# Gate's v with tokens stationary: rounded products of 512 features for the prompt, float32 visits for the samples

## The chip, the cores and the metric

One core of one Trainium2 chip runs the whole kernel. The time is device microseconds (us) of one execution; the median of three runs counts. A profile is one execution of its own, with its own time.

## What is computed

One inference step of a decoder layer for 256 prompt tokens and 64 sample tokens (8 sequences of 8), in float32. The tokens lie side by side as 320 columns. What concerns us is the first projection and the gate's v:

```python
h = rms_norm(x, p["norm_mix_pre"])
proj = h @ p["w_in"]                      # 2048 -> 9248 columns
a_u, a_v, z, xbc, dt_raw = ...            # a_v: 2048 columns
v = layer_norm(jax.nn.gelu(a_v, approximate=False), ln_g, ln_b)
...
s = jnp.einsum("hts,bnshd->bnthd", w, vp) + b_s
return u * s, v[:, start:]
```

v is needed with a token in each partition and its 2048 features along the row: the layer norm runs over the features, and the gate's product sums over tokens. After the mixer come a projection back, a norm, and a convolved feed-forward layer (2048 to 2 x 5632 and back to 2048) with a last norm and residual.

## The kernel before, in words

**Products.** A float32 weight block (a "slab", `slab`, L109) is loaded on SyncE's queue, rounded to float32r by ScalarE (`whi`, L124), and what the rounding lost is taken by VectorE (`wlo`, L125). The tokens are split in the same way into `hT[0]` and `hT[1]`. A product is then three float32r products: whi x hi, whi x lo, wlo x hi (`accumulate`, L132, its matmuls at L136 to L138). The weight block of 128 features is stationary and the 320 tokens move, so a result has features in the partitions and tokens along the row. 16 row blocks of 128 inputs (kt, `KD` = 16) are summed in one PSUM bank. Two pools hold the eight banks: `mm` with four, `ms` (`misc`) with four. Rounded weights have three buffers each (`whi`, `wlo`), raw slabs three (`wraw`).

**The first visit.** At the start nothing is loaded yet, so the kernel begins with ten products of ones (L69) and goes through kt from 0 to 15 with six feature blocks of v at once (768 columns, L684 on): four banks of `mm` and two of `ms`. For each kt the tokens are split (`x_ready`, L614, on ScalarE and VectorE), for kt below 4 the slab comes in two halves of 384 columns, and in between run the squares of x (`x_squares`), the loads for dt and, at kt 15, the root of the mean square (`root`, L633: token sums on TensorE at L638 and L640, then eleven small steps on VectorE) and the products for dt (`dt_products`, L492, at L497). The other ten feature blocks of v follow as three calls of `project` (L743 to L745).

**Turning v.** As features lie in the partitions, v has to be turned. `v_out` (L649) turns each finished bank in 32x32 blocks on VectorE (L653), and for each pair of blocks GpSimd's queue writes the turned rows to memory (L657). `v_in` (L663) is a side task: it loads the rows back by tokens on GpSimd's queue (L671), ScalarE applies the gelu with the token's root as its scale (L675) and writes `vt`, and VectorE gathers the statistics of the layer norm (L678). `layer_norm` (L747) waits until this task is done.

**Order.** The instructions of each engine stand in the order of the program except where a priority or `tc.issue_after` says otherwise; `tick` (L159) lets background tasks emit their next step between products, by counts of products made. `last_made` is the newest product on TensorE; with `issue_after(last_made[0])` an instruction stays behind it in its engine's order.

**The form that the change takes up.** In the down projection of the feed-forward layer the tokens are stationary already: `prompt_products` (L1509, matmul at L1513) has 128 tokens stationary and 512 rounded weight columns moving; `sample_products` (L1516, matmul at L1520) takes the 64 sample tokens unrounded, as true float32, against the raw weights, two products side by side in the two halves of the array's columns (`tile_position=(0, 64 * h)`). `samples()` calls it four times, with four products in each call.

**The end.** The last part of the down projection (`down_plain`, L1665) adds each finished bank to the sums (`joined`, L1671) on VectorE, takes squares on ScalarE, multiplies by the last norm's gain on GpSimd (`by_pool`, L1823) or VectorE (`by_gain`, L1815), and writes the result when a token's root is there. `last_sum` (L1833) is one more addition on VectorE; `one_block` (L1847) says which engine takes which gain. All of VectorE's steps there stand in the order of the code. Helpers record these steps at one line, L1806 for VectorE and L1810 for ScalarE.

Of the kernel before, what the change touches and what calls it, by code (L numbers as in the profile page):

```python
# [8 lines left out]
F32 = mybir.dt.float32  # L9
# [7 lines left out]
P = 128  # L17
NP = 256
# [15 lines left out]
def hybrid_step(  # L34
# [394 lines left out]
    with ExitStack() as mctx:  # L429
# [160 lines left out]
        with tc.tile_pool(name="gp", bufs=1) as gp:  # L590
# [23 lines left out]
            def x_ready(k0, nk):  # L614

                with tc.high_priority(offset=100000), tc.issue_after(rounded[0]) if rounded else nullcontext():
                    for kt in range(k0, k0 + nk):
                        x = xf[:, kt, :]
                        x_split.append(act.activation(hT[0][:, kt, :], x, AF.Copy, scale=pre[:, kt:kt + 1]).ins)
                        x_low.append(dve.scalar_tensor_tensor(out=hT[1][:, kt, :], in0=x, scalar=pre[:, kt:kt + 1],  # L620
                                                              in1=hT[0][:, kt, :].bitcast(F32), op0=ALU.mult, op1=ALU.subtract).ins)
# [25 lines left out]
            v_there = []  # L647

            def v_out(b, ps):  # L649

                t = turned[b // 2 % len(turned)]
                with first():
                    dve.transpose(out=t[:, :, b % 2], in_=ps[:, :NT].rearrange("p (s f) -> p s f", f=32))  # L653
                if b % 2:
                    for i in range(4):
                        rs = slice(32 * i, 32 * i + 32)
                        pool.dma_start(v_d[b // 2][:, 64 * i:64 * i + 64].rearrange("(s t) e -> t s e", t=32),  # L657
                                       t[rs].rearrange("p s j f -> p s (j f)"))
                    v_there.append(b // 2)

            bn = [gp.tile([P, 4, 6], F32, name=f"bn{c}") for c in range(3)]

            def v_in():  # L663

                for a in range(KD // 2):
                    while a not in v_there:
                        yield 24, 0
                    rows = []
                    for c, (o, n) in enumerate(TOK):
                        rows.append(tp.tile([P, NT], F32, tag="pv", name="v_rows", bufs=4)[:, :2 * P])  # L670
                        pool.dma_start(rows[c][:n], v_d[a][o:o + n])  # L671
                    yield 48, 0
                    with tc.issue_after(last_made[0]):
                        for c, (o, n) in enumerate(TOK):
                            func_ins.append(act.activation(vt[:n, c, 2 * P * a:2 * P * a + 2 * P].rearrange("p (j i f) -> p j i f", j=2, f=32),  # L675
                                                           rows[c][:n].rearrange("p (i j f) -> p j i f", j=2, f=32), AF.Gelu, scale=r[:n, c:c + 1]).ins)
                            if a % 2:
                                dve.bn_stats(bn[c][:n, a // 2, :], vt[:n, c, 256 * a - 256:256 * a + 256])  # L678
                    yield 0, 0
                with tc.issue_after(func_ins[-1]):  # L680
                    act.activation(held, ones[:, 0:1], AF.Silu)

            dt_loads = []
            ps = [mm.tile([P, 512], F32, tag="mm", name=f"ps_v{j}") for j in range(4)] + [misc(f"ps_v{j}") for j in (4, 5)]  # L684
            for kt in range(KD):
                x_ready(kt, 1)
                x = [h[:, kt, :] for h in hT]
                if kt < 4:
                    for g in range(2):
                        wb = slab(rows_of(w_in, kt, 1, V0 + 384 * g, 384), g, begins=kt + g == 0)  # L690
                        if kt == 0:
                            made_so_far[0] += 9
                            for i in (0, 2, 1):
                                for j in range(3):
                                    pe.matmul(ps[3 * g + j][:, :NT], wb(0, j)[i // 2], x[i % 2], start=i == 0, stop=False)
                        else:
                            for j in range(3):
                                accumulate(ps[3 * g + j][:, :NT], wb(0, j), *x, False, False)
                else:
                    wb = slab(rows_of(w_in, kt, 1, V0, 768))  # L700
                    for j in range(6):
                        accumulate(ps[j][:, :NT], wb(0, j), *x, False, kt == KD - 1)
                if 6 <= kt < 14:
                    with tc.issue_after(x_split[-1]):
                        x_squares(2 * (kt - 6))
                if kt in (8, 10):
                    dt_loads.append(dt_columns(kt // 10, gp))
                    next(dt_loads[-1])
                if kt in (12, 14):
                    with tc.issue_after(x_low[-1]):  # L710
                        next(dt_loads.pop(0), None)
                if kt == 15:
                    r = root()
                if kt == 15:
                    dt_products()
                if kt == 14:

                    with tc.issue_after(rounded[0]):
                        act.activation(held, ones[:, 0:1], AF.Gelu)
            turned = [gp.tile([P, 4, NT], F32, tag="vf", name="turned", bufs=2).rearrange("p j n -> p (j n)") for _ in range(2)]  # L720
            turned = [t[:, 2 * NT * h:2 * NT * h + 2 * NT].rearrange("p (s j f) -> p s j f", j=2, f=32) for t in turned for h in range(2)]
            for j in range(6):
                v_out(j, ps[j])
            for t, src in ((a_bc, ssm_a_log), (bias_bc, ssm_dt_bias)):

                pool.tensor_copy(t[:, 0:1], hT[0][:, 13, 0:1].bitcast(F32))
# [11 lines left out]
                next(tasks)  # L738
                yield 24, 0
            bg.append(with_r1())  # L740
            v_task = v_in()
            side.append(v_task)
            project(w_in, V0 + 768, lambda j, ps: v_out(6 + j, ps))  # L743
            project(w_in, V0 + 1280, lambda j, ps: v_out(10 + j, ps))
            project(w_in, V0 + 1792, lambda j, ps: v_out(14 + j, ps), width=256)  # L745

            def layer_norm():  # L747

                mv = gp.tile([P, 3, 2], F32, name="mv")
                pool.memset(mv, 1.0)  # L750
                while v_task in side:
                    yield 24, 0
# [558 lines left out]
    with tc.tile_pool(name="fp", bufs=1) as fp:  # L1311
# [353 lines left out]
        def down_plain(ck, parts, done, others):  # L1665
# [55 lines left out]
            for nb, i, w in sorted(later, key=lambda t: t[:2])[:-2]:  # L1721
                if i == 0:
                    ps = mm.tile([P, 512], F32, tag="mm", name=f"pd_{nb}_0")
                prompt_products(ps, x_of_tokens(0, i), w, i == 0, i == 1, True)
                if (nb, i) == (1, 1):
                    dve_add(f[0][1], ps)
                    samples_summed()
                    root(2, 0)
                    one_block(0, 1)
                    by_gain(2, 1)  # L1730
                    root(2, 1)
                    result(2, 0)
# [260 lines left out]
```

## Time and profile before

| | us |
|---|---|
| median of three runs | 1733.81 |
| lowest and highest | 1733.52, 1733.90 |
| the profiled execution | 1732.14 |
| its span in the trace | 1730.4 |
| busy: TensorE, VectorE, ScalarE, GpSimd | 1721.5, 1336.2, 878.6, 667.0 |

TensorE's granted clock was 0.999 over the span. How to read the lines that follow: a timeline row is start, duration, engine, line, operation, output and inputs with shapes; in brackets the idle time of the engine before it and what ended it. A row of the chain of waits is start, the time that it holds of the chain, and what. A row of the list of waits is who waited for whom, the total in us, how often, and the longest. Matmuls overlap in the pipeline, so the duration of one is longer than the distance to the next; distances of starts are the price. Rows of windows give, for each stretch, busy us (and instructions) of TensorE, its weight loads, VectorE, ScalarE and GpSimd, then the granted clock, the share of the DMA engines and GB/s.

### The profile page before, as it was taken

The numbers are of one execution on the slowest core, as the hardware profiler recorded it, in microseconds if no ns is written. First come the engines' busy times: TensorE is split into PE (matmuls) and PEld (weight loads), VectorE is DVE, ScalarE is ACT, GpSimd is POOL, SyncE is SP. The second block draws the span as 40 slices with busy tenths as digits, with TensorE's granted clock in tenths as the row PEclk, the third lists the DMA queues.
The fourth block names the chain that finished last, engine by engine and source line by source line (L and its number), as shares of the span: only waits on it lengthen the run. The fifth ranks groups of instructions, "written<-read, shape, count | busy, mean of one in ns | idle before, by whom it ended". The sixth has DMA issues, their size and how long they took to land.

```text
span 1730.4 us, 29959 instructions
## 1 busy us (share of the span) xinstructions
PE 1721.5 (99%) x11239; PEld 1608.1 (93%) x11239; DVE 1336.2 (77%) x2138; ACT 878.6 (51%) x1277; POOL 667.0 (39%) x1018
## 2 busy tenths in 40 slices
PE   9999999999999999999999999999999999999998
PEld 9999999999999999999998988989898989898985
DVE  7548864657869788788988878778787878697898
ACT  6344554333656565645655544444454544454554
POOL 2532230000414323112256546464545464555552
PEclk9999999999999999999999999999999999999999
DMA  8776655556676777665766454554545454545445
GB/s 263 219 236 189 186 173 152 156 161 186 204 227 198 227 218 218 203 208 165 224 190 216 122 177 136 170 153 155 165 143 161 138 170 135 174 134 172 135 152 156
DMA packets 216129, 310.07 MB, mean 179 GB/s; under 512 B 22064, under 2 KB 118960, under 8 KB 215792
## 3 DMA queue, kind: packets, MB, share of 16 engines
q1 hardware_dynamic: 198912, 280.02, 53.4%
q0 software_dynamic: 6144, 13.35, 2.7%
q10 hardware_dynamic: 10928, 14.79, 2.5%
q8 instruction: 88, 1.44, 0.3%
q14 instruction: 57, 0.47, 0.1%
HBM read 284.47 MB, written 22.32 MB: 177 GB/s over the span
## 4 chain that ended last, share of the span: by engine, by line
PE 98%; DVE 1%; DMA 0%; issue 0%; ACT 0%; DVEq 0%; SPq 0%; ACTq 0%
PE ps L136 21%; PE ps L138 20%; PE ps L137 20%; PE pm L1513 11%; PE pd L136 4%; PE pd L137 4%; PE pd L138 4%; PE pms L1520 4%; PE y_ps L1089 1%; PE ps_v L137 1%; PE ps_v L136 1%; PE ps_v L138 1%; PE yo_ps L1004 0%; PE up_ps L1021 0%; PE sg L811 0%; PE pd L1513 0%
## 5 line engine op out<-in xcount | busy, mean ns | idle before, releaser
L136 PE MATMUL ps<-h_hi,whi 128*128 128x320 f32 x2428 | 750.3, 309 | 0.0
L137 PE MATMUL ps<-h_lo,whi 128*128 128x320 f32 x2428 | 748.5, 308 | 0.0
L138 PE MATMUL ps<-h_hi,wlo 128*128 128x320 f32 x2428 | 748.3, 309 | 0.0
L125 DVE TENSOR_TENSOR wlo<-wraw,whi 128x1024 fp32r<-128x1024 f32 (+2 forms) x394 | 487.5, 1238 | 147.6 <-ACT whi L124 145.6
L124 ACT CAST whi<-wraw 128x1024 fp32r<-128x1024 f32 (+2 forms) x393 | 405.5, 1033 | 372.0 <-PE ps L137 143.8
L136 PEld LDWEIGHTS ps<-h_hi,whi 128*128 128x128 f32 x2428 | 455.6, 188 | 9.7 <-issue 1.3
L137 PEld LDWEIGHTS ps<-h_lo,whi 128*128 128x128 f32 x2428 | 455.9, 188 | 6.4
L138 PEld LDWEIGHTS ps<-h_hi,wlo 128*128 128x128 f32 x2428 | 455.5, 188 | 0.3
L136 PE MATMUL pd<-ohi,whi 128*128 128x320 f32 x448 | 138.7, 310 | 0.0
L138 PE MATMUL pd<-ohi,wlo 128*128 128x320 f32 x448 | 138.3, 309 | 0.0
L137 PE MATMUL pd<-olo,whi 128*128 128x320 f32 x448 | 138.3, 309 | 0.0
L1528 ACT CAST whi<-b 128x1024 fp32r<-128x1024 f32 x50 | 52.4, 1047 | 77.2 <-PE ps L137 56.6
L1376 POOL COPY ptf<-pad 128x2 f32<-128x2 f32 x88 | 41.8, 475 | 122.0 <-DVE pad L1358 120.3
L1529 DVE TENSOR_TENSOR wlo<-b,whi 128x1024 fp32r<-128x1024 f32 x50 | 65.2, 1303 | 29.6 <-ACT whi L1528 29.6
L136 PEld LDWEIGHTS pd<-ohi,whi 128*128 128x128 f32 x448 | 84.1, 188 | 0.6
L137 PEld LDWEIGHTS pd<-olo,whi 128*128 128x128 f32 x448 | 84.1, 188 | 0.3
L138 PEld LDWEIGHTS pd<-ohi,wlo 128*128 128x128 f32 x448 | 84.1, 188 | 0.0
L1551 POOL TENSOR_TENSOR one<-b,one 128x256 f32<-128x256 f32 x80 | 78.0, 1006 | 4.9 <-DVE wlo L1529 4.7
L249 DVE TENSOR_TENSOR acc_mix<-acc_mix,pd 128x320 f32<-128x320 f32 (+1 forms) x113 | 53.9, 480 | 28.2 <-PE pd L138 28.1
L1529 DVE TENSOR_TENSOR wlo<-one,whi 128x1024 fp32r<-128x1024 f32 x40 | 55.8, 1394 | 22.8 <-ACT whi L1528 22.7
L1520 PE MATMUL pms<-b,a_s 128*64 128x512 f32 x280 | 70.9, 596 | 0.0
L1528 ACT CAST whi<-one 128x1024 fp32r<-128x1024 f32 x40 | 41.8, 1045 | 57.0 <-PE ps L137 54.1
(447 smaller groups left out, 2811.1 us busy)
## 6 DMA issues: line engine op xcount, KB each, us to landing
wraw<-in_ffn_w_up SPq DMA_DIRECT2D x176, 512.0 KB, 3.8
wraw<-in_w_in SPq DMA_DIRECT2D x132, 512.0 KB, 3.9
b<-in_ffn_w_down SPq DMA_DIRECT2D x70, 512.0 KB, 5.4
wraw<-in_w_out SPq DMA_DIRECT2D x64, 512.0 KB, 3.5
st<-in_state_ssm SPq DMA_DIRECT2D x40, 256.0 KB, 4.5
out_ssm_state_sample<-st ACTq DMA_DIRECT2D x30, 256.0 KB, 2.5
cs<-dacs_d SPq DMA_DIRECT2D x16, 320.0 KB, 5.6
in_mix<-in_ffn_w_down SPq DMA_DIRECT2D x10, 512.0 KB, 4.1
```

The lines of the kernel that those rows point to most:

```text
L124: rounded[:] = [act.copy(hi, raw).ins]
L125: lowered[:] = [dve.tensor_tensor(out=lo, in0=raw, in1=hi.bitcast(F32), op=ALU.subtract).ins]
L136: pe.matmul(ps, whi, xhi, start=first, stop=False)
L137: pe.matmul(ps, whi, xlo, start=False, stop=False)
L138: last_made[0] = pe.matmul(ps, wlo, xhi, start=False, stop=last).ins
L249: added_last[:] = [dve.tensor_tensor(out=acc[:, nb, ts], in0=acc[:, nb, ts], in1=ps[:, ts], op=ALU.add).ins]
L1376: with tc.issue_after(pool.tensor_copy(ptf[:, k, :], pad[:, 256:258]).ins):
L1513: last_made[0] = pe.matmul(ps, x[xi][:, k], w[wi][:, 512 * k:512 * k + 512], start=start and k + i == 0, stop=stop and k == 1 and i == 2).ins
L1520: last_made[0] = pe.matmul(ps[64 * h:64 * h + 64], a_s[:, k0 + k], w[h][:, 512 * k:512 * k + 512], start=start and k == 0, stop=stop and k ...
L1528: rounded[:] = [act.copy(hi, raw).ins]
L1529: dve.tensor_tensor(out=lo, in0=raw, in1=hi.bitcast(F32), op=ALU.subtract)
L1551: pool.tensor_tensor(out=room[:, cs], in0=raw[x][:, cs], in1=raw[y][:, cs], op=ALU.subtract)
```

## The change

v is now made with tokens stationary, in two halves of 1024 features (`v_of(0)` and `v_of(1)`), each over all 16 kt. A prompt bank holds 128 tokens by 512 features; four `mm` banks (two token blocks c, two feature blocks h) are summed at once, and one `misc` bank takes the samples, both feature blocks in its two halves. The raw slabs stay until the samples' products have used them: seven rooms, the three `wraw` buffers and four that lie idle at this time. After every fourth kt a visit makes the samples' products of four row blocks, eight of them. The last two kt are made bank by bank, so that a bank is finished while the next is still worked on. The gelu then reads the banks (`v_rows`), with the token's root as its scale; turning, the way through memory and the side task are gone. `x_s` is a new copy of the sample columns of x, scaled, on ScalarE (64 columns for each kt).

```diff
-    v_d = [dr.tile([NT, 2 * P], F32, name=f"v_d{i}") for i in range(KD // 2)]
...
+                        act.activation(x_s[:, kt], xf[:, kt, NP:], AF.Copy, scale=pre[:, kt:kt + 1])
...
-            def v_out(b, ps):
...
-            def v_in():
...
+            raw_rooms = [t.rearrange("p j n -> p (j n)")[:, :1024] for t in
+                         (bT, cT, *(hp.tile([P, 4, NT], F32, tag=t, name="v_raw") for t in ("ohi", "olo")))]
+            def v_slab(n, kt):
+                at = slabs[0] % 7
+                slabs[0] += 1
+                room = raw_rooms[at - 3] if at >= 3 else None
+                halves = 2 if n == 0 and kt < 4 else 1
+                for g in range(halves):
+                    slab(rows_of(w_in, kt, 1, V0 + 1024 * n + 512 * g, 1024 // halves), g, begins=n + kt + g == 0, room=room)
+                return tuple(both)
+            def v_products(ps, kt, c, w, hs=(0, 1)):
+                for xi, wi in ((0, 1), (0, 2), (1, 1)):
+                    for h in hs:
+                        last_made[0] = pe.matmul(ps[c, h], hT[xi][:, kt, P * c:P * c + P], w[wi][:, 512 * h:512 * h + 512],
+                                                 start=kt + xi == 0 and wi == 1, stop=kt == KD - 1 and xi == 1).ins
+                        made_so_far[0] += 2
+            def v_samples(ps, raws):
+                for kt in sorted(raws):
+                    for h in range(2):
+                        with tc.issue_after(last_made[0]):
+                            last_made[0] = pe.matmul(ps[64 * h:64 * h + 64], x_s[:, kt], raws[kt][:, 512 * h:512 * h + 512], start=kt == 0,
+                                                     stop=kt == KD - 1, tile_position=(0, 64 * h)).ins
+            def v_rows(n, c, h, ps):
+                r, q = roots_of_x[0], 2 * n + h
+                rows = slice(64 * h, 64 * h + 64) if c == 2 else slice(0, P)
+                to = vt[:NS, 2] if c == 2 else vt[:, c]
+                func_ins.append(act.activation(to[:, 512 * q:512 * q + 512], ps[rows], AF.Gelu, scale=r[rows, c:c + 1]).ins)
+                dve.bn_stats(bn[c][:to.shape[0], q, :], to[:, 512 * q:512 * q + 512])
+            def v_of(n):
+                ps = {(c, h): mm.tile([P, 512], F32, tag="mm", name=f"ps_v{c}{h}") for h in range(2) for c in range(2)}
+                ps_s, raws, last = misc("ps_vs"), {}, []
+                for kt in range(KD):
+                    if n == 0:
+                        x_ready(kt, 1)
+                    w = v_slab(n, kt)
+                    raws[kt] = w[0]
+                    if kt < KD - 2:
...
+                            for c in range(2):
+                                v_products(ps, kt, c, w)
+                    else:
+                        last.append(w)
+                    if kt % 4 == 3 and kt < KD - 1:
+                        v_samples(ps_s, raws)
+                        raws.clear()
...
+                for h in range(2):
+                    for c in range(2):
+                        for i, w in enumerate(last):
+                            v_products(ps, KD - 2 + i, c, w, (h,))
+                        if n + h + c == 0:
+                            roots_of_x.append(root())
+                            dt_products()
+                        v_rows(n, c, h, ps[c, h])
+                v_samples(ps_s, raws)
+                for h in range(2):
+                    v_rows(n, 2, h, ps_s)
+            v_of(0)
...
-            project(w_in, V0 + 768, lambda j, ps: v_out(6 + j, ps))
-            project(w_in, V0 + 1280, lambda j, ps: v_out(10 + j, ps))
-            project(w_in, V0 + 1792, lambda j, ps: v_out(14 + j, ps), width=256)
+            v_of(1)
...
-                while v_task in side:
-                    yield 24, 0
```

For the very first kt the four banks are taken in turn for each pair of parts (whi x hi: h = 0 for both token blocks, then h = 1), and in `v_of(1)` each kt ends with `tick()`. The squares, the loads for dt and the table for the gelu stand at the same kt as before.

Two small edits lie at the end of the kernel, in the last part of the down projection. The addition of bank (1, 1) and `last_sum` move behind VectorE's `wlo` of the sixth slab, and the gain of block (0, 1) moves from GpSimd to VectorE, behind the results of the samples:

```diff
+                        if n == 5:
+                            with tc.issue_after(lowered[0]):
+                                joined(1, 1, second)
+                                last_sum()
...
-                            if i == 1:
+                            if i == 1 and (c, nb) != (1, 1):
                                 joined(c, nb, ps[nb, c])
-                                if (c, nb) == (1, 0):
-                                    last_sum()
+                            elif i == 1:
+                                second = ps[nb, c]
...
                     result(2, 1)
+                    by_gain(0, 1)
...
-            elif (c, nb) in ((0, 0), (0, 1), (1, 2)):
+            elif (c, nb) in ((0, 0), (1, 2)):
                 by_pool(c, nb)
```

More of the change, by code (lines that the diff above doesn't have):

```diff
@@ L645, in hybrid_step @@
                 .rearrange("p (k n) -> p k n", n=NH)
-            v_there = []
-            def v_out(b, ps):
[L651 to L659, printed above, removed]
@@ L661, in hybrid_step @@
-            bn = [gp.tile([P, 4, 6], F32, name=f"bn{c}") for c in range(3)]
-            def v_in():
-                for a in range(KD // 2):
-                    while a not in v_there:
-                        yield 24, 0
[L668 to L695, printed above, removed]
-                        else:
[L697 to L723, printed above, removed]
+            x_s = op.tile([P, 4, NT], F32, tag="xs", name="x_s", bufs=2).rearrange("p j n -> p (j n)")[:, :KD * NS]\
+                .rearrange("p (k n) -> p k n", n=NS)
@@ new lines, in hybrid_step @@
+            bn = [gp.tile([P, 4, 6], F32, name=f"bn{c}") for c in range(3)]
+            raw_rooms = [t.rearrange("p j n -> p (j n)")[:, :1024] for t in
+                         (bT, cT, *(hp.tile([P, 4, NT], F32, tag=t, name="v_raw") for t in ("ohi", "olo")))]
+            dt_loads, slabs, roots_of_x = [], [0], []
+            def v_slab(n, kt):
[6 more added lines that the diff above has]
+                return tuple(both)
@@ new lines, in v_rows @@
+            def v_rows(n, c, h, ps):
[13 more added lines that the diff above has]
+                    if kt < KD - 2:
+                        if n + kt == 0:
+                            for xi, wi in ((0, 1), (0, 2), (1, 1)):
+                                for h in range(2):
+                                    for c in range(2):
+                                        pe.matmul(ps[c, h], hT[xi][:, 0, P * c:P * c + P], w[wi][:, 512 * h:512 * h + 512],
+                                                  start=xi == 0 and wi == 1, stop=False)
+                                        made_so_far[0] += 2
+                        else:
+                            for c in range(2):
[5 more added lines that the diff above has]
+                        raws.clear()
+                    if n == 1:
+                        tick()
+                        continue
+                    if 6 <= kt < 14:
+                        with tc.issue_after(x_split[-1]):
+                            x_squares(2 * (kt - 6))
+                    if kt in (8, 10):
+                        dt_loads.append(dt_columns(kt // 10, gp))
+                        next(dt_loads[-1])
+                    if kt in (12, 14):
+                        with tc.issue_after(x_low[-1]):
+                            next(dt_loads.pop(0), None)
+                    if kt == 14:
+                        with tc.issue_after(rounded[0]):
+                            act.activation(held, ones[:, 0:1], AF.Gelu)
+                for h in range(2):
+                    for c in range(2):
+                        for i, w in enumerate(last):
[5 more added lines that the diff above has]
+                v_samples(ps_s, raws)
+                for h in range(2):
+                    v_rows(n, 2, h, ps_s)
@@ L724, in hybrid_step @@
+            v_of(0)
+            r = roots_of_x[0]
             for t, src in ((a_bc, ssm_a_log), (bias_bc, ssm_dt_bias)):
@@ L740, in hybrid_step @@
             bg.append(with_r1())
-            v_task = v_in()
-            side.append(v_task)
-            project(w_in, V0 + 768, lambda j, ps: v_out(6 + j, ps))
-            project(w_in, V0 + 1280, lambda j, ps: v_out(10 + j, ps))
-            project(w_in, V0 + 1792, lambda j, ps: v_out(14 + j, ps), width=256)
+            v_of(1)
+            with tc.issue_after(func_ins[-1]):
+                act.activation(held, ones[:, 0:1], AF.Silu)
             def layer_norm():
@@ L750, in layer_norm @@
                 pool.memset(mv, 1.0)
-                while v_task in side:
-                    yield 24, 0
                 for c, (o, n) in enumerate(TOK):
```

## The prediction

> **What bounds the kernel now.** I read the page first, then the list of waits of TensorE, then the timeline of TensorE at three places, and last the other engines where the change touches them.
>
> ```profile
> span 1730.4 us, 29959 instructions
> ...
> PE 98%; DVE 1%; DMA 0%; issue 0%; ACT 0%; DVEq 0%; SPq 0%; ACTq 0%
> ```
>
> The page: TensorE holds 98% of the chain that ended last. A busy TensorE need not be a fast one, so the question is how much of that is waiting in disguise.
>
> ```profile
> PE last_result L1896 <- DVE unread L1806: 2.4, 1, 2.4
> PE early L69 <- DVE ones L65: 1.1, 1, 1.1
> PE pd L1513 <- DVE wlo L125: 0.3, 1, 0.3
> ```
>
> The waits of TensorE (total, times, longest): three in the whole run, 3.8 us, and none of them in Gate's v. Nothing that the change takes off VectorE, ScalarE, GpSimd or the queues in that stage can be worth more than what TensorE waits for there, which is nothing. So the change is priced by TensorE's own time, product by product.
>
> ```profile
> 8.06 0.31 PE L136 MATMUL ps_v<-h_hi,whi 128*128 128x320 f32 x1
> ...
> 23.90 0.31 PE L136 MATMUL ps_v<-h_hi,whi 128*128 128x320 f32 x1
> ```
>
> Here is the rate of the old products. The 0.31 us is how long one is in flight, not its price: they overlap. Between these two starts lie 36 triples, 108 products, in 15.84 us: 0.1467 us each for 320 columns, 0.458 ns a column.
>
> **The change, part by part. Removed products.** Gate's v is 2048 features in 16 blocks of 128, times 16 row blocks (kt), times three products: 768 x 0.1467 = 112.6 us, all on the path.
>
> **Prompt products.** New: 2 halves of the features x 16 kt x 2 token blocks x 2 blocks of 512 features x 3 = 384 products, with 128 tokens stationary and 512 weight columns moving. The down projection already makes that form (L1513). It stands in the chain of waits (start, time, what) beside the float32 products of the samples (L1520):
>
> ```profile
> 912.94 7.02 PE pms L1520 x32
> 919.96 1.59 PE pm L1513 x6
> ```
>
> ```profile
> 963.09 1.39 PE pm L1513 x6
> ```
>
> Six cost 1.39 us, 0.2317 us each; the rate per column of the old form would give 512 x 0.458 = 0.2347. I take the middle, 0.2332: 384 x 0.2332 = 89.5 us (89.0 to 90.1).
>
> **Sample products.** New: 2 halves x 16 kt x 2 blocks of 512 = 64 products of unrounded float32, 64 tokens stationary, two side by side in the halves of the array. L1520 is exactly this form. How many products is "x32"? The code makes 4 calls of 4 products there, 16; and a single call of 4 near the end (1694.33, below) stands as x8. So one float32 product leaves two records, and a product costs 7.02 / 16 = 0.439 us. 64 x 0.439 = 28.1 us. The Trainium skill (FP8 and Floating Point Precision, TensorE Precision Notes) says that true float32 takes four passes through the array; by it, with two products side by side, one would cost two passes of 0.2347, 0.469 us, and the 64 of them 30.0 us. The trace's 0.439 is 1.87 such passes, so rule and row nearly meet; the row stands in the sum.
>
> **Edges of the visits.** The samples come in 8 visits of 8 products. What does changing form cost? After the long visit six prompt products take 1.59 instead of 1.39 us: 0.20. A short one, of 4 products, in the timeline of TensorE:
>
> ```profile
> 1694.00 0.39 PE L1513 MATMUL pd<-kept,a_hi 128*128 128x512 f32 x1
> 1694.33 1.94 PE L1520 MATMUL pds<-raw,a_s 128*64 128x512 f32 x8
> 1696.19 0.50 PE L1513 MATMUL pd<-whi,a_hi 128*128 128x512 f32 x1
> 1696.53 0.40 PE L1513 MATMUL pd<-whi,a_lo 128*128 128x512 f32 x1
> ...
> 1718.05 0.28 PE L1745 MATMUL pd<-whi,a_hi 128*128 128x256 f32 x1
> ...
> 1720.77 0.28 PE L1745 MATMUL pd<-held_w,a_hi 128*128 128x256 f32 x1
> ```
>
> From 1694.00 to 1696.53 are 2.53 us, less two prompt products (0.47) and four sample products (1.76): 0.30. Eight visits: 1.6 to 2.4, I take 2.0.
>
> TensorE in all: -112.6 + 89.5 + 28.1 + 2.0 = **+7.0 us** (+6.1 to +8.0). The prompt's share of the old products, 256 of 320 columns, was 90.1 us and stays what it was; the samples' share was 22.5 us and becomes 30.1.
>
> **The start.** The first visit's slabs grow from 768 to 1024 columns, its halves from 384 to 512, and with tokens stationary the first row block needs the second half's rounded weights after two products instead of after nine.
>
> ```profile
> 4.29 0.56 ACT L619 ACTIVATE h_hi<-vt 128x320 fp32r<-128x320 f32 x1 [1.05 <-DMA vt<-in_xT]
> ...
> 5.41 0.51 ACT L124 CAST whi<-wraw 128x384 fp32r<-128x384 f32 x1 [0.56 <-DMA vt<-in_xT]
> ```
>
> ```profile
> 5.33 0.69 PE L695 MATMUL ps_v<-h_hi,whi 128*128 128x320 f32 x3
> ```
>
> ```profile
> 6.00:8.00 2.00, 2.00 (x16) 2.00 (x15) 1.53 (x3) 1.41 (x4) 1.28 (x5) 1.00 1.09 374
> ```
>
> The second half's rounding starts at 5.41 and the first product at 5.33. In the new order it is wanted at 5.33 + 2 x 0.23 = 5.8. Ahead of it on ScalarE's queue now stands the new copy of the sample columns (an estimate, 0.25 us: 64 columns of a step whose 320 take 0.56), and the rounding itself grows from 0.51 to an estimated 0.65: 5.66 + 0.65 = 6.3, so 0.5 us late, if its load has landed. The window's row has the DMA engines full (share 1.09, 374 GB/s), and 128 KB more by then are 0.35 us at that rate, all of the queues together, or about 0.9 at half of it. So 0 to 2.5 us over the first row blocks; I take **+1.0**.
>
> **Edits with one answer, 0.** Rounding of weights, and what hides it (timeline of VectorE, one row block of the first visit):
>
> ```profile
> 21.04 0.96 DVE L125 TENSOR_TENSOR wlo<-wraw,whi 128x768 fp32r<-128x768 f32 x1 [0.68 <-ACT whi L124]
> 21.92 0.55 DVE L620 SCALAR_TENSOR_TENSOR h_lo<-vt,h_hi 128x320 fp32r<-128x320 f32 x1
> 22.38 0.82 DVE L631 TENSOR_TENSOR acc_mix<-acc_mix 128x640 f32<-128x640 f32 x1
> ```
>
> The rounding of 1024 columns takes 1.23 us (at 1704.40, below). A row block of the first half costs VectorE 1.23 + 0.55 + 0.82 = 2.6 us at most, against 12 x 0.233 = 2.80 us of TensorE and 0.9 more for its share of a visit. It is hidden by little where squares are summed; were a visit's cover gone, a row block could lose 0.1 to 0.2. The turning on VectorE, v's way out and back on GpSimd's queue and its late gelu go: worth 0, nobody on the path waited for them. The seven rooms for raw slabs are freed four at a visit, and the first is wanted again three row blocks (8.4 us) later.
>
> **The handover of the banks.** This wait is new. The old gelu read rows from memory; now it reads the banks, so the second half of the features can't write its first bank until the first half's gelu has, and that needs the root.
>
> ```profile
> 50.55 0.15 DVE L261 TENSOR_SCALAR rs_v<-tsum 128x3 f32<-128x3 f32 x1
> ...
> 52.51 0.16 DVE L267 SCALAR_TENSOR_TENSOR rs_r<-rs_t,rs_r 128x3 f32<-128x3 f32 x1
> ```
>
> ```profile
> 48.37 2.29 PE ps_dt L497 x32
> ```
>
> ```profile
> 1711.17 0.61 ACT L1810 ACTIVATE unread<-in_mix 128x512 f32<-128x512 f32 x1
> ```
>
> The root is 2.1 us of small steps, behind perhaps two roundings (2.5). A gelu of 128x512 is nearest to the square of that shape, 0.61. From the token sums: 4.6 + 0.6, so the first bank is free after 5 to 6 us, and the third, wanted second, after at most 9 with two casts in between. Before it needs them, TensorE has three banks' last products (18 x 0.233 = 4.2), the products for dt and a visit (8 x 0.439 + 0.25 = 3.8): 10.3 us. Cost 0; if the root came 5 us later, each further us would cost one. Queued behind a waiting product on TensorE is everything, so this is the rival to watch.
>
> **The end.** Two edits in the last down projection.
>
> ```profile
> 1700.72 0.69 DVE L1806 TENSOR_TENSOR in_mix<-in_mix,pd 128x512 f32<-128x512 f32 x1
> 1701.32 1.51 DVE L125 TENSOR_TENSOR wlo<-wraw,whi 128x1024 fp32r<-128x1024 f32 x1
> ...
> 1704.40 1.23 DVE L125 TENSOR_TENSOR held_w<-raw,held_w 128x1024 fp32r<-128x1024 f32 x1 [0.43 <-ACT held_w L124]
> ...
> 1716.92 1.19 DVE L1806 SCALAR_TENSOR_TENSOR last_n<-last_s,last_r 128x1 f32<-128x1 f32 x1
> ```
>
> ```profile
> 1716.80 1.29 POOL L1825 TENSOR_TENSOR in_mix<-in_mix,gain 128x512 f32<-128x512 f32 x1 [3.15 <-ACT unread L1810]
> ```
>
> The sum at 1700.72 moves behind the rounding at 1701.32, which ends TensorE's 0.3 us wait; but the next rounding, at 1704.40, waits for ScalarE and is wanted soon after, so perhaps 0.15 stays. The multiplication on GpSimd at 1716.80 goes; beside it a step of one column took 1.19 us, where the steps of the root above take 0.16, which frees 1.03 on VectorE's last chain, and the same multiplication takes about 0.69 there, as the sum of that shape at 1700.72 does. Together -0.5 (-0.9 to 0).
>
> **Sum:** +7.0 + 1.0 - 0.5 = +7.5 us. The profiled execution took 1732.14 us (span 1730.4 and 1.74 around it) and becomes 1739.6. The median of the runs, 1733.81, lies 1.67 above it; with that kept, **1741.3 us**.
>
> **The rivals.**
> *Faster: a float32 product costs one record.* Place: the eight visits. If a sample product of this kernel cost 7.02 / 32 = 0.219 us, they would take 14.0 us, and the time would be 1741.3 - 14.1 = 1727.2. The sign turns at 0.439 - 7.5/64 = 0.32 us a product. For it: the chain's count taken at its word. Against it: 16 products of the code for 32 records, and 4 for 8. Chance 0.03.
> *No change: a fixed part in every product.* 768 products become 384 (and 64), and if each carried a fixed part F beside its columns, fewer and longer ones would win it back: a prompt product would cost (0.1467 - F) x 512/320 + F, 0.6 F less than by columns alone. To bring the loss under 3.5 us, 384 x 0.6 F must reach some 4.6 us: F = 20 ns, and the time 1737. For it: 0.2317 is a little under 0.2347. Against it: from 1718.05 to 1720.77 above are 23 steps of 256 columns, 0.118 us each, 0.46 ns a column like the 320 and the 512, which leaves at most 5 ns. Chance 0.05, with all else that would halve the loss. The Trainium skill has such a part and speaks for this change by it (TensorEngine Tiling (Array Packing), Instruction Overhead: about 60 cycles a matmul); an estimate from that page, 25 ns, would give 1736; the rows above don't show it.
> *Slower still: a wait in the new order* (bank, or first loads, or VectorE's thin margin). For it: no such wait is in the trace of before, and the margins are thin. 3 to 5 us more: 1744 to 1746. Chance 0.15.
> *It doesn't do what it says:* the prompt's products could only shrink if columns were saved, and 384 x 512 is the 768 x 256 of before; nothing there is left to save.
>
> **How the numbers follow.** Forecast 0.77. What a measurement can tell from no change is 0.2%, 3.5 us: below 1730.3 or above 1737.3. The bounds give 1733.8 + 6.1 - 0.9 = 1739.0 to 1733.8 + 8.0 + 2.5 = 1744.3; I reach up to 1746 for the wait and down to 1737.5. Faster 0.03, same 0.06, slower 0.91.
>
> **What would show it.** In the changed profile: 384 products at about 0.233 us from start to start, 128 float32 records at 0.219, the v stage ending some 8 us later than the 122 us of before, no new row in TensorE's waits but one under 2 us in the first 10 us, and the step of one column near the end back at 0.16. Wrong would be: a wait on a gelu or on the root, sample products under 0.32 us, or prompt products under 0.22.

## The result, and the profile after

The changed kernel takes 1745.27 us in the median of five runs (1744.13 to 1745.99). The kernel before took 1733.63 in five runs on the same chip (1732.54 to 1733.90). The ratio is 1.0067, with a 95% interval of 1.0056 to 1.0079: slower by 11.6 us. The prediction was 1741.3, in a range of 1737.5 to 1746.0. So the sign and the range held, and the forecast's own sum is 4 us short. The profiled execution took 1745.27 us, against 1732.14 before.

First the page:

```profile
span 1743.6 us, 29312 instructions
...
PE 96%; DVE 2%; DMA 1%; issue 0%; ACT 0%; POOL 0%; DVEq 0%; SPq 0%; ACTq 0%
```

There are 647 instructions fewer, and the time is longer. TensorE still carries nearly the whole chain, so the loss has to be looked for there: in products that cost more, or in waits. The list of TensorE's waits (who for whom; total in us, times, longest) shows the second kind:

```profile
PE last_result L1915 <- DVE unread L1825: 2.0, 1, 2.0
PE ps L136 <- ACT whi L124: 1.5, 2, 1.3
...
PE ps L136 <- DVE pad L450: 0.9, 1, 0.9
PE ps L136 <- DVE room L450: 0.5, 1, 0.5
PE pd L1527 <- DVE held_w L125: 0.4, 1, 0.4
PE pd L1527 <- DVE wlo L125: 0.3, 1, 0.3
```

Before, there were three rows. The three with L136 are new, and so is the one for `held_w`, at the very end of the kernel. None of them is in Gate's v and none waits for a gelu or the root. Those with L136 stand, but for 0.2 us, in the projection that follows v. The chain of waits leads through v to the place (start, time, what):

```profile
17.16 3.58 PE ps_vs L677 x16
20.74 11.36 PE ps_v L669 x48
...
58.39 2.29 PE ps_dt L496 x32
60.68 4.39 PE ps_v L669 x18
65.07 3.58 PE ps_vs L677 x16
68.65 2.99 PE ps_v L669 x12
...
125.18 3.61 PE ps_vs L677 x16
128.81 0.68 ACT vt L684
129.52 0.57 ACT vt L684
130.23 1.05 ACT whi L124
131.33 0.41 PE ps L136
```

L669 is the prompt's products and L677 the samples'. Until 128.8 everything lies on TensorE: 48 prompt products in 11.36 us, a visit of eight sample products (16 records) in 3.58. Nothing in it waits, at the change of the banks (60.68 to 71.6) either. Then the chain leaves TensorE for two gelus and a rounding of weights, and comes back at 131.33. Around that place, the windows of 5 us (busy us of TensorE, its weight loads, VectorE, ScalarE, GpSimd; granted clock; DMA share; GB/s):

```profile
115.00:120.00 5.00, 5.00 (x23) 4.05 (x22) 1.23 (x1) 1.05 (x1) 0.00 (x0) 1.00 0.00 0
120.00:125.00 5.00, 5.00 (x23) 3.86 (x21) 1.85 (x3) 2.06 (x3) 0.00 (x0) 1.00 0.00 0
...
130.00:135.00 5.00, 3.67 (x15) 3.46 (x16) 4.89 (x11) 4.93 (x8) 1.50 (x4) 0.69 0.54 172
135.00:140.00 5.00, 5.00 (x35) 5.00 (x35) 2.91 (x6) 2.60 (x3) 0.48 (x1) 0.97 0.91 253
```

For ten us before the end of v the DMA engines move nothing at all, with a whole projection's weights still to come. And after it TensorE is granted 0.69 of its clock. The timeline of SyncE's queue says when the next weights were asked for, that of ScalarE when they were rounded, and that of TensorE what it cost:

```profile
111.29 0.33 SPq L118 DMA_DIRECT2D bT<-in_w_in  x1
126.23 11.06 SPq L118 DMA_DIRECT2D wraw<-in_w_in  x6
```

```profile
128.81 1.39 ACT L684 ACTIVATE vt<-ps_vs,rs_r 64x512 f32<-64x512 f32 x2 [2.91 <-PE ps_vs L677]
130.23 1.04 ACT L124 CAST whi<-wraw 128x1024 fp32r<-128x1024 f32 x1
```

```profile
128.70 1.30 PE L510 MATMUL dt_ps<-sums,dtf 128*128 128x32 f32 x10
131.33 0.41 PE L136 MATMUL ps<-h_hi,whi 128*128 128x320 f32 x1 [1.33 <-ACT whi L124]
...
164.43 0.39 PE L136 MATMUL ps<-h_hi,whi 128*128 128x320 f32 x1 [0.94 <-DVE pad L450]
...
166.03 0.39 PE L136 MATMUL ps<-h_hi,whi 128*128 128x320 f32 x1 [0.48 <-DVE room L450]
```

The load after 111.29 is issued at 126.23, 15 us later, and goes to `wraw`. v's 32 raw slabs take the seven rooms in turn from number 0, so the last four lie in rooms 0 to 3: the three `wraw` buffers and bT. A raw slab is freed by the visit that reads it, and the last visit starts at 125.18. The next projection loads into `wraw` alone. Its first weights therefore can't be asked for until v is all but done. ScalarE, which has nothing left to round, is idle for 2.91 us until the samples' bank is finished; then the two gelus come, and the first rounding behind them. In the gap TensorE does five tiny float32 products for dt (ten records).

How to cost a half clock from such rows: 5 us at 0.69 are 5 x (1 - 0.69) / 0.5 = 3.1 us at half, 0.3 more in the next window: 3.4 us, in which 1.7 us of work are lost.

### The profile page after: what moved, and what is told of

The parts are those of the page before. It is cut to its first block, busy times and chain, and to the rows that moved or that the text cites. A ratio compares the mean times of both kernels' runs of the same rounds, so it can differ in the third digit from the quotient of the medians.

```text
span 1743.6 us, 29312 instructions
## 1 busy us (share of the span) xinstructions
PE 1731.9 (99%) x10983; PEld 1577.0 (90%) x10983; DVE 1329.3 (76%) x2119; ACT 878.0 (50%) x1276; POOL 641.9 (37%) x961
## 4 chain that ended last, share of the span: by engine, by line
PE 96%; DVE 2%; DMA 1%; issue 0%; ACT 0%; POOL 0%; DVEq 0%; SPq 0%; ACTq 0%
PE ps L136 19%; PE ps L138 18%; PE ps L137 18%; PE pm L1527 11%; PE ps_v L669 5%; PE pd L136 4%; PE pd L137 4%; PE pd L138 4%; PE pms L1534 4%; PE ps_vs L677 2%; PE y_ps L1103 1%; PE yo_ps L1018 0%; PE up_ps L1035 0%; PE sg L825 0%; DMA raw<-in_ffn_w_down 0%
## 5 line engine op out<-in xcount | busy, mean ns | idle before, releaser
L136 PE MATMUL ps<-h_hi,whi 128*128 128x320 f32 x2268 | 702.2, 310 | 3.0 <-ACT whi L124 1.5
L137 PE MATMUL ps<-h_lo,whi 128*128 128x320 f32 x2268 | 700.3, 309 | 0.0
L138 PE MATMUL ps<-h_hi,wlo 128*128 128x320 f32 x2268 | 699.5, 309 | 0.0
L125 DVE TENSOR_TENSOR wlo<-wraw,whi 128x1024 fp32r<-128x1024 f32 (+1 forms) x372 | 464.7, 1250 | 132.4 <-ACT whi L124 130.9
L124 ACT CAST whi<-wraw 128x1024 fp32r<-128x1024 f32 (+1 forms) x371 | 386.3, 1042 | 350.9 <-PE ps L137 118.7
L136 PEld LDWEIGHTS ps<-h_hi,whi 128*128 128x128 f32 x2268 | 426.2, 188 | 13.0 <-issue 2.9
L137 PEld LDWEIGHTS ps<-h_lo,whi 128*128 128x128 f32 x2268 | 426.5, 188 | 6.4
L138 PEld LDWEIGHTS ps<-h_hi,wlo 128*128 128x128 f32 x2268 | 425.9, 188 | 0.5 <-DVE wlo L125 0.2
L136 PE MATMUL pd<-ohi,whi 128*128 128x320 f32 x448 | 139.0, 310 | 0.0
L136 PEld LDWEIGHTS pd<-ohi,whi 128*128 128x128 f32 x448 | 84.1, 188 | 0.6
```

The costliest lines, as they stand in the source:

```text
L124: rounded[:] = [act.copy(hi, raw).ins]
L125: lowered[:] = [dve.tensor_tensor(out=lo, in0=raw, in1=hi.bitcast(F32), op=ALU.subtract).ins]
L136: pe.matmul(ps, whi, xhi, start=first, stop=False)
L137: pe.matmul(ps, whi, xlo, start=False, stop=False)
L138: last_made[0] = pe.matmul(ps, wlo, xhi, start=False, stop=last).ins
```

## The experiments

Where no other is named, a run is compared with the kernel before on the same chip, 1732.74 us for e1 to e4 and 1733.00 for e5 and e6. The last two come from another chip. The theory after the result: v's own work costs what was predicted (+7), and the other 4 to 5 us come from the late load at the end of v. Rivals: sample products dearer than priced, dearer edges of the visits, the end of the kernel.

**e1, the rooms.** The count starts at the fourth room, so that the last four slabs lie in the four rooms which are idle anyway, and `wraw` is free early:

```diff
-            dt_loads, slabs, roots_of_x = [], [0], []
+            dt_loads, slabs, roots_of_x = [], [3], []
```

> The changed kernel with one number changed: the count that chooses the rooms of the raw slabs starts at 3 instead of 0, so that the last four slabs of v lie in the four borrowed rooms and the three wraw buffers are free for the next projection's slabs before v ends. Theory (late load): the wait of TensorE after v (1.5 us), the half clock behind it (1.7 us) and the two waits on bank evacuation at 164 to 166 us (1.8 us) all follow from the next slab's load being held back by the last visit; then all three go, 5 us, and the time is 1740.3 us. Rival (queue): the next slab's rounding only stands behind the last gelus in ScalarE's queue; then another room changes nothing, 1745 us. Second rival (VectorE full): the first two go but the waits at 164 to 166 us stay, as the layer norm still runs there: 1742 us.

Measured: 1740.47 us (1739.79 to 1741.25), ratio 1.0043 (1.0028 to 1.0057). The waits of TensorE, the chain at the end of v, SyncE's queue, and the window with the half clock:

```profile
PE last_result L1915 <- DVE unread L1825: 2.0, 1, 2.0
...
PE ps L136 <- DVE pad L450: 0.9, 1, 0.9
PE ps L136 <- ACT whi L124: 0.2, 1, 0.2
```

```profile
125.41 3.58 PE ps_vs L677 x16
128.99 0.34 PE ps L136
```

```profile
112.37 23.63 SPq L118 DMA_DIRECT2D wraw<-in_w_in  x7
```

```profile
130.00:135.00 5.00, 5.00 (x36) 5.00 (x35) 5.00 (x13) 2.98 (x4) 0.77 (x2) 1.00 0.53 192
```

The loads start 14 us earlier, the products of the next projection follow the visit at once, the clock stays at 1.00, and 4.8 us are back (3.9 when each kernel is taken against its own runs of before). It is one number in the code, with the same work on every engine, so where the last slabs lie is shown as the cause of what went at this place: the wait of 1.33, the half clock and the wait of 0.48, some 3.6 us. About 0.8 more went at the end of the kernel, where this profile has no wait for `held_w` and `wlo`; the rooms don't touch that place (see e2). The expectation was met in part only: the other wait for VectorE's reading of a bank (L450), 0.9 us, stays.

The first rival, the gelus in ScalarE's queue, would have left the time at 1745, and it didn't stay there. The order on ScalarE did move together with the loads, for three roundings now stand ahead of the last gelus; but in the changed kernel the loads of this place took at least 3.8 us from issue to landing, so the one issued at 126.23 landed at about 130.0 at the earliest, and the gelus can have held the rounding at 130.23 back by no more than 0.2 us.

**e2, the end alone.** The kernel before with nothing but the two edits in the last down projection:

```diff
+                        if n == 5:
+                            with tc.issue_after(lowered[0]):
+                                joined(1, 1, second)
+                                last_sum()
...
+                    by_gain(0, 1)
...
-            elif (c, nb) in ((0, 0), (0, 1), (1, 2)):
+            elif (c, nb) in ((0, 0), (1, 2)):
```

> The kernel before with the two edits at the end alone. Prediction's term: -0.5 us (-0.9 to 0), 1733.1. Rival: the edits shorten VectorE's last chain by 0.4 us (the step of one column at 0.16 instead of 1.19 us) but the last slabs' landing sets the rounding, so that nothing is left of the other 0.3 us: -0.4 or less. Slower by more than 0.3 us would mean that the later sum delays a later rounding.

Measured: 1733.14 us, ratio 0.9998 (0.9988 to 1.0007): no change that can be told, and the interval (-2.1 to +1.2 us) can't tell the -0.5 of the prediction from nothing either. So the profile has to say what happened. The waits of TensorE, then the rounding of the slab in question on ScalarE and on VectorE:

```profile
PE last_result L1901 <- DVE unread L1811: 2.0, 1, 2.0
...
PE pd L1513 <- DVE held_w L125: 0.5, 1, 0.5
```

```profile
1705.67 1.05 ACT L124 CAST held_w<-raw 128x1024 fp32r<-128x1024 f32 x1 [1.10 <-DMA raw<-in_ffn_w_down]
```

```profile
1706.75 1.23 DVE L125 TENSOR_TENSOR held_w<-raw,held_w 128x1024 fp32r<-128x1024 f32 x1 [1.05 <-ACT held_w L124]
```

The wait of the last result is 0.4 shorter than before (2.4), as it should be. The wait for `wlo` (0.3) went, but the next slab's rounding (`held_w`) is now waited for, 0.5. Together these rows give 0.2 us, far below what can be measured. The moved sum isn't what holds `held_w` back: VectorE stands idle for 1.05 us before it, until ScalarE has its part, and ScalarE stands idle for 1.10 until the slab has landed. That is the rival of the expectation, the last slabs' landing. The same edits are in e1, e3 and e4, and there neither wait is left.

**e3, few sample products.** e1 with the sample products of kt 0 and 15 alone, 8 in the place of 64; v's sample rows are then incomplete.

```diff
-                    for h in range(2):
+                    for h in range(2 if kt in (0, KD - 1) else 0):
```

> e1_rooms with only 8 of the 64 float32 sample products (kt 0 and 15; the sample rows of v are left incomplete). Theory (a product leaves two records and costs 0.439 us): 56 x 0.439 = 24.6 us and four visits' edges of 0.27 less, 25.7 us under e1_rooms. Rival (one record a product, 0.219 us): 13.4 us under it. If a visit is hidden behind something else: less than 12 us.

Measured: 1724.75 us (1724.15 to 1725.27), ratio 0.9952 (0.9938 to 0.9966), 15.7 less than e1: between what the two theories gave, so by itself it decides nothing. The profile shows why. Waits of TensorE, and two windows:

```profile
PE ps_v L669 <- ACT whi L124: 2.5, 2, 1.8
PE ps_v L669 <- DVE wlo L125: 2.3, 4, 0.8
```

```profile
50.00:55.00 5.00, 3.63 (x9) 2.21 (x9) 3.73 (x6) 3.00 (x4) 0.41 (x2) 0.50 0.35 105
55.00:60.00 5.00, 5.00 (x39) 2.05 (x39) 2.48 (x12) 0.69 (x1) 0.00 (x0) 0.54 0.02 3
```

Without the visits the first half of v is no longer bound by TensorE. Loading, splitting and rounding fall behind, and the clock goes to half for about 10 us, in which TensorE is busy for 8.3; that loses 4.2. With the price that e5 finds below, 56 products at 0.429 and the edges of the four visits that are gone, at 0.3, are 25.2; less 4.8 of waits and 4.2 of clock that is 16.2, against the 15.7 measured. So taking work away was a poor way to price it: the work had been the cover of something else. e5 does it the other way round.

**e4, visits twice as often.** e1 with a visit after every second kt: 16 visits of four products in the place of 8 of eight.

```diff
-                    if kt % 4 == 3 and kt < KD - 1:
+                    if kt % 2 == 1 and kt < KD - 1:
```

> e1_rooms with visits after every second kt: 16 visits of four products instead of 8 of eight. The work is the same, eight more changes of form. Theory (an edge costs 0.25 to 0.3 us of TensorE): 2.0 to 2.4 us over e1_rooms. Rival (the edge is a matter of long visits only, or is hidden): within 0.5 us of e1_rooms.

Measured: 1744.28 us (1744.10 to 1744.65), ratio 1.0065 (1.0049 to 1.0081), 3.8 more than e1. One visit and the products around it in the chain:

```profile
21.01 5.79 PE ps_v L669 x24
26.80 1.87 PE ps_vs L677 x8
28.66 5.80 PE ps_v L669 x24
```

A period is 7.66 us: 24 prompt products (5.60) and four sample products leave 0.3 for the edges, as the prediction had from its one short visit. v ends 2.7 us later by that. A further 0.8 is lost at the waits for VectorE in the projection behind v (1.5 us of waits at L450 where e1 has 0.9); the remaining 0.3 is smaller than what the same code differs by from one profile to the next.

**e5, the sample products twice.** e1 with each visit's products made a second time, into a bank that nothing reads:

```diff
+                ps_s, ps_t, raws, last = misc("ps_vs"), misc("ps_again"), {}, []
...
                         v_samples(ps_s, raws)
+                        v_samples(ps_t, raws)
```

> The kernel of e1 (1740.47 us) with every visit's sample products made a second time, into a bank that nothing reads: 64 more float32 products, no new load, rounding, bank reader or change of form beyond one switch of bank in each visit. The theory (a product of 512 features with a column half is done in 0.439 us, the two records of the trace being halves of one product): 64 x 0.439 = +28.1, near 1768.6. The rival (one record is one product, 0.219 us each): +14.0, near 1754.5. If part of the 3.58 us of a visit were not products but fixed edges, the visit of eight would grow by less than 3.51 us, and the time by less than 28.

Measured: 1766.39 us (1765.83 to 1767.97), ratio 1.0194 (1.0177 to 1.0211), 25.9 more than e1 (25.7 with each taken against its own runs of before). The chain through one visit:

```profile
16.89 3.58 PE ps_vs L677 x16
20.48 3.43 PE ps_again L677 x16
23.91 11.36 PE ps_v L669 x48
```

The second eight take 3.43 us, 0.429 each. The first eight take 0.15 more, which is the edge into the visit. 64 x 0.429 = 27.4: the price of 0.439 was right to a few per cent, and one record per product (14.0) is refuted. The first product of the next projection starts 26.9 us later than in e1, and e1's wait of 0.9 at L450 isn't there in e5, so some 26 are left; the measured 25.9 agrees within the two intervals.

**e6, one product at a time.** e1 with both feature halves in the same column half of the array, to two banks:

```diff
-                            last_made[0] = pe.matmul(ps[64 * h:64 * h + 64], x_s[:, kt], ...
-                                                     stop=kt == KD - 1, tile_position=(0, 64 * h)).ins
+                            last_made[0] = pe.matmul(ps[h][0:64], x_s[:, kt], ...
+                                                     stop=kt == KD - 1, tile_position=(0, 0)).ins
```

> The kernel of e1 (1740.47 us) with the two feature halves of a sample product in the same column half of the array, to two banks, so that no two of them can be in the array side by side; everything else stays. The theory (two column halves run side by side, four passes of 512 columns each, and the pair takes 2 x 0.439 = 0.878 us because the second costs almost nothing beside the first): alone a product takes between 0.878 us and four rounded passes, 4 x 0.2334 = 0.934 us, so 64 of them cost 56.2 to 59.8 in the place of 28.1: +28.1 to +31.7, near 1768.6 to 1772.2. The rival (a float32 product of 512 features takes 0.439 us wherever it stands, and the halves don't overlap): no change, near 1740.5.

Measured: 1767.15 us (1766.05 to 1769.31), ratio 1.0197 (1.0182 to 1.0213), 26.7 more than e1 (26.4 with each taken against its own runs of before). That is near the theory and below its range of 28.1 to 31.7, and far from the rival's 0. The chain within a visit:

```profile
17.51 1.00 PE ps_vs L677 x2
18.51 0.86 PE ps_vt L677 x2
19.37 0.86 PE ps_vs L677 x2
```

A product by itself takes 0.86 us, a little under the lower bound of 0.878, and twice 0.429, so side by side the second of a pair costs nothing. 64 products would add 64 x 0.429 = 27.4; as in e5, e1's wait of 0.9 at L450 isn't there. The Trainium skill (TensorE: Matmul & The Clock Gate, Why this matters for your kernels, the row on small-M matmuls) says that products in distinct column groups run concurrently; the pair here is a clean case of it. And the four passes that the prediction took from the skill (FP8 and Floating Point Precision, TensorE Precision Notes) agree if a pass is 0.86 / 4 = 0.214 us; the prediction's estimate of 30.0 us was too high only because it took the slower rounded product (0.2347) for a pass.

No run was faster than the kernel before with the whole of the work done: with every wait gone the new v would still take more of TensorE than the old.

## Why the prediction was right, and where it was not

By its own steps, from the profiles:

| step | predicted, us | measured, us |
|---|---|---|
| TensorE's own work in v | +7.0 | +7.2 |
| the start | +1.0 | +0.1 |
| the handover of the banks | 0 | 0 |
| edits with one answer: the rooms | 0 | +3.6 |
| edits with one answer: VectorE's other work | 0 | +0.9 |
| the end | -0.5 | 0 |
| sum | +7.5 | +11.8 (the medians differ by 11.6, the two profiled executions by 13.1) |

Of the 1.3 us by which the profiled executions differ beyond the sum, only a part is placed: the products behind the waits at 164 and 166 start 1.1 and 0.6 us later than they would have, where the rows of idle time say 0.94 and 0.48. In e1 the same steps are +7.3, +0.2, 0, 0, +0.9 and -0.8, together 7.6, against 7.7 between its median and that of the kernel before.

That the measured 1745.3 lies in the range is luck in part: the sum's own bounds ended at 1744.3, and the range had been stretched to 1746 for a wait of another kind than the one that came.

**Own work: right, in its parts too.** From the first product (5.42) to the end of v (128.70, where the products for dt start that follow it) are 123.3 us. In the kernel before, the first product of the next projection stands here:

```profile
121.42 0.31 PE L136 MATMUL ps<-h_hi,whi 128*128 128x320 f32 x1
```

From 5.33 that is 116.1 us. Token sums, products for dt and the spread of the root (0.34 + 0.21 + 2.29 + 0.33) are the same in both; without them v's products went from 112.9 to 120.1 us. Product and edge were each a little off and their sum was not: eight products and their edges were priced 3.51 + 0.25, and e5 has 3.43 + 0.15 into the visit and about as much out of it. The 7.02 us from which the price of 0.439 came held the edge into that visit as well (16 x 0.429 + 0.15 = 7.01).

**The two rivals on the price fell.** One record per product is refuted by e5. The fixed part in every product isn't seen: the prompt product costs 0.233, and v's own work came out 0.2 over the sum, not 4 below it. So here the trace decides against the rule of 60 cycles a matmul (the Trainium skill, TensorEngine Tiling (Array Packing), Instruction Overhead), taken as a part that is added to every product.

**The start was over-priced.** The first product starts at 5.42 against 5.33, and the waits have no new row in the first 10 us. Range 0 to 2.5, value 1.0, truth near its lower end. The second half's weights were wanted soon, but they were there.

**The bank handover was right.** The root and the gelu came in time: the last of the four gelus that free the prompt's banks ends at 67.0, and the second half's first product starts at 68.65.

**The failed step** is the sentence on the rooms among the edits with one answer: seven rooms "are freed four at a visit, and the first is wanted again three row blocks (8.4 us) later". It holds within v, where somebody always has a free room. It wasn't followed to the last visit, where the next user is another loop that knows only three of the rooms. The prediction asked what the moved loads wait for, not who waits for the buffers that they hold last. Of the 3.6, 1.33 is the wait for the first rounded weights, 1.74 the half clock behind it (17 products in 4.23 us, which take 2.49 at the full clock), and 0.48 the second wait for VectorE, at 166; in e1 all three are gone. The sign that the prediction gave, no new row in TensorE's waits but one in the first 10 us, failed with it.

The other wait for VectorE, 0.94 at 164, is as long in e1; it is the 0.9 of the table. The chain of waits of e1 leads back from it, through VectorE's and ScalarE's roundings, to the load of one of the layer norm's rows (`lb`):

```profile
149.44 4.65 DMA lb<-in_gate_ln_b
...
158.21 1.23 DVE wlo L125
...
160.05 0.39 PE ps L136
```

VectorE stands idle for 1.6 us until this row has landed, and the rounding and the reading of the bank stand behind it in VectorE's order. The profiles agree on it: the changed kernel, e1, e3 and e4 all have the wait of TensorE, and in all four VectorE waits 1.6 to 1.9 us in all for `lb`; the kernel before, e5 and e6 don't have it, and there VectorE waits 0.3 us at most. No run moved this load, so it is read from the profiles and not shown by an experiment, and why the load comes late is open. In the changed kernel two more steps of VectorE stand in the same chain, one for dt (L521, 1.13 us), whose products TensorE did early, in the gap, and one for the gate (L811, 0.62 us); in e1 neither stands there, and the second wait is gone.

The rival "slower still" thus came true in size (1744 to 1746) with a chance of 0.15, by a wait of the new order at none of the three places that it named.

**The end: the mechanism was right and the gain didn't reach the time of the changed kernel.** The step of one column is at 0.17 again, and the last result waits 2.0 us where it waited 2.4. But `held_w`, for which the prediction had given 0.15, is waited for 0.4 us in the changed kernel and 0.5 in e2. In the changed kernel a wait for `wlo` of 0.3 is there as well; it isn't the old one, which ended with the rounding from `wraw` (1701.32), but one for the next slab, rounded from `raw`. Both follow the landing of the last slabs: ScalarE waits for the load of `held_w`'s slab 0.4 us in the changed kernel and 1.1 in e2, and in the changed kernel 1.05 for the slab before it. In e1, e3 and e4, with the same edits, TensorE waits for neither, and its waits at the end are 0.8 us shorter than before. The landing differs from one profile to the next, and the prediction had sized it from a single one.

## What to carry to other kernels

A change that keeps buffers longer has to be followed past its own stage: ask which buffers it holds last, who wants them next, and whether that one can use any others. A stretch in which the DMA engines move nothing while weights are still to come is the sign of it in the profile. When a float32 product is to be priced, double it with a result that nobody reads; leaving it out can take away cover and price something else.

## What the hardware showed that was not expected

A short gap cost more than itself. TensorE stood idle for 1.33 us behind 1.3 us of very small products (128.70 to 130.0), and the clock was then at half for 3.4 us, which is another 1.7. The Trainium skill (TensorE: Matmul & The Clock Gate, Part 1: The HAM clock gate) has the clock judged in windows of about 3.4 us, and the length of the half clock agrees with one such window. Its advice to leave no gap above about 3 us (Why this matters for your kernels) is too generous for this case: the gap here is 2.6 us with the small products counted. In e3 a stretch with several short waits (1.8 us the longest) was enough for 10 us at half clock.

The pass of a float32 product, 0.214 us for 512 columns, if four passes are counted, is shorter than a rounded (float32r) product of the same width, 0.233. No run here says why.
